# A softplus series moved to VectorE, an early table load and four longer delays in a hybrid layer

## The chip, the cores and the metric

The kernel runs on one NeuronCore of a Trainium2 chip. The metric is device time in microseconds (us), the median of repeated executions. A profile is one execution taken by the hardware profiler.

## The reference

One layer of a hybrid model for 512 prompt tokens and 64 sampled tokens (8 sequences of 8), width 1024, in float32. Three mixers share one input projection: a gated delta rule (4 heads), a differential attention (4 heads) and a pooling mixer. A convolutional feed-forward network follows. Cut to what the change touches:

```python
h = rmsnorm(x, norm_mix)
proj = jnp.einsum('bld,de->ble', h, w_in)
aq, ak, av, az, aa, ab, bq, bk, bv, cx = split_cols(proj, IN_WIDTHS)
qkv, new_conv = causal_dwconv(jnp.concatenate([aq, ak, av], axis=-1), conv_buf, a_conv_w, a_conv_b)
qkv = jax.nn.silu(qkv)
g = -jnp.exp(a_log) * jax.nn.softplus(aa + a_dt_bias)
beta = jax.nn.sigmoid(ab)
o_a, new_delta = gated_delta_rule(q, k, v, g, beta, delta_s0)
# differential attention: softmax of two score maps, their difference times v
mixed = jnp.concatenate([o_a, o_b, o_c], axis=-1)
x = x + jnp.einsum('ble,ed->bld', mixed, w_out)
f, new_ffn = conv_ffn(rmsnorm(x, norm_ffn), ffn_buf, ffn_up, ffn_conv_w, ffn_conv_b, ffn_down)
```

The softplus is max(y, 0) + log(1 + exp(-|y|)). The kernel works out the logarithm as a series: with t = exp(-|y|) and z = t / (t + 2), it is 2z (1 + z²/3 + z⁴/5 + ... + z¹⁶/17).

## The kernel before

**Gemms.** All 576 tokens stand as columns. Each float32 product is three fp32r products of high and low parts: `w_hi` with the high part of x, `w_hi` with its low part, `w_lo` with its high part, each in two pieces of 256 and 320 columns. "A product" in this text is one such matmul. A weight block of 512 KB is fetched by SyncE (`w_raw`), rounded to `w_hi` by ScalarE (line 174) and subtracted to `w_lo` by VectorE (line 175). A gemm result (`g`) has one of two PSUM buffers.

**The order of TensorE** is written by hand. The gemms form the main stream. Side work is written as generators. A virtual clock adds a time for every matmul, and a generator that yields a number is taken up again when that clock has advanced by so many nanoseconds. So a yield says how many products stand between two pieces of side work. All matmuls are kept in program order. On VectorE, ScalarE, GpSimd and SyncE a scheduler orders the instructions by its own simulated timeline, except where the program pins them.

**The start** (`first_products`, lines 334 to 382). x comes in four pieces of two row tiles. For each piece ScalarE makes `wide` (hi) and VectorE its low part; ScalarE squares it (`sq`) and VectorE adds the squares into `total`. The first two weight blocks come in a small part (two row tiles) and the rest. TensorE runs 16 matmuls on ones at the very start, then 96 products of the first two output tiles, then five small matmuls of `total` with ones (the token sums), then products with `wab`, the weights of the decay. From the token sums come `r5`, five diagonal tiles `dg`, `rstd`, and with it everything behind the projection.

**The decays** (`decays`, lines 462 to 506). From a 128x20 tile y the series above is worked out, then `gt`, which TensorE multiplies with triangular constants. Exponentials of the results (`dec`, `gsum`) gate the delta rule. `gsum` goes through device memory (`gsum_d`) into the tile `XT` of each head. The polynomial is a loop of seven multiply-and-add pairs on GpSimd (lines 483 and 484). `yield 11000` stands in front of the matmuls of `gt`.

**The fronts** (`front`, line 553 on), one per delta head: transposes of k, squares into `kt`, a yield, transposes of q and v, then five products of k with k and q whose results VectorE scales into `U`.

**The inversion and the levels** (`invert`, line 611; `levels`, line 647). All heads' 32x32 blocks are inverted on VectorE in 31 multiply-and-subtract pairs (lines 631 and 633). The result goes through device memory (`inv`) and comes back per head as `Xc`. VectorE transposes it into `XTc`, which has one buffer, and four ScalarE copies put it into the diagonal of `XT` (line 666). Two heads at a time, TensorE multiplies `Xc` with `U` into `Y`, and after a yield `Y` with `XT`, whose negated results ScalarE copies into `X64` and `XT` (line 651).

**The attention values** (`values`, line 963): one to four transposes of a score tile, a ScalarE copy `wt` (line 970), a yield, then the products with v. The psm pool has four banks for all side work.

Of the kernel before, what the change touches and what calls it, by code (L numbers as in the profile page):

```python
# [9 lines left out]
F32 = mybir.dt.float32  # L10
F32R = mybir.dt.float32r
AF = mybir.ActivationFunctionType
ALU = mybir.AluOpType
AX = mybir.AxisListType

P = 128
D = 1024
KT = D // P
NP = 512
NS = 64  # L20
T = NP + NS
# [38 lines left out]
def hybrid_step(ctx: ExitStack, tc: tile.TileContext, I, O):  # L60
    nc = tc.nc
# [185 lines left out]
    epst = const.tile([P, 20], F32, name="mhalf")  # L247
# [12 lines left out]
    def col(nm, i):  # L260
        return par[:, off[nm] + i:off[nm] + i + 1]
# [24 lines left out]
    sp = startstack.enter_context(tc.tile_pool(name="start", bufs=1, side="right", reuse_waits="tile"))  # L286
    xs = [sp.tile([P, 2, T], F32, name=f"x{j}") for j in range(KT // 2)]
    raws = []

    def load_first(queue, parts):  # L290

        for w in range(2):
            if len(raws) <= w:
                raws.append((wp.tile([P, 8, P], F32, name="w_raw"), next(sources)))
            raw, src = raws[w]
            queue.dma_start(raw[:, parts], src[:, parts])
# [4 lines left out]
    load_first(nc.scalar, slice(0, 2))  # L301
    load_first(nc.sync, slice(2, 8))
# [32 lines left out]
    def first_products():  # L335
# [4 lines left out]
        def split_first(r):  # L340
            for w in range(2):
                nc.scalar.copy(his[w][:, r], raws[w][0][:, r])  # L342
                nc.vector.tensor_sub(los[w][:, r], raws[w][0][:, r], his[w][:, r].bitcast(F32))  # L343

        ps = [psg.tile([P, 1024], F32, name="g") for _ in range(2)]
        total = None
        for j in range(KT // 2):
            if j < 2:
                split_first((slice(0, 2), slice(2, 8))[j])
            for k in (2 * j, 2 * j + 1):  # L350
                x = xs[j][:, k % 2]
                hi, lo = hmix[k]
                nc.scalar.activation(hi, x, AF.Identity, scale=col("norm_mix", k))
                last_lo[0] = nc.vector.scalar_tensor_tensor(lo, x, col("norm_mix", k), hi.bitcast(F32),
                                                            op0=ALU.mult, op1=ALU.subtract).ins
                for w in range(2):
                    for i, (a, b) in enumerate(((his, hi), (his, lo), (los, hi))):
                        for r in PARTS:
                            mm(ps[w][:, O0:O1][:, r], a[w][:, k], b[:, r], start=k + i == 0,
                               stop=k == KT - 1 and i == 2)  # L360
            sq = sp.tile([P, 2, T], F32, name="sq", bufs=2)
            nc.scalar.activation(sq.rearrange("p k t -> p (k t)"), xs[j].rearrange("p k t -> p (k t)"), AF.Square)
            if total is None:
                total = sp.tile([P, T], F32, name="total")
                nc.vector.tensor_add(total, sq[:, 0], sq[:, 1])
            else:
                for k in range(2):
                    nc.vector.tensor_add(total, total, sq[:, k])
# [92 lines left out]
    def decays(abT):  # L461
# [11 lines left out]
        z = ab.tile([P, 5, HEADS], F32, name="z")  # L473
# [3 lines left out]
        nc.gpsimd.tensor_scalar_add(t2, t1, 2.0)  # L477
        nc.vector.reciprocal(t2, t2)
        nc.gpsimd.tensor_mul(z, t1, t2)
        nc.gpsimd.tensor_mul(z2, z, z)  # L480
        nc.vector.tensor_scalar(t1, z2, 1.0 / 17, 1.0 / 15, op0=ALU.mult, op1=ALU.add)
        for d in (13, 11, 9, 7, 5, 3, 1):
            nc.gpsimd.tensor_mul(t1, t1, z2)  # L483
            nc.gpsimd.tensor_scalar_add(t1, t1, 1.0 / d)  # L484
        nc.vector.scalar_tensor_tensor(t1, t1, 2.0, z, op0=ALU.mult, op1=ALU.mult)
# [7 lines left out]
        yield 11000  # L493
# [17 lines left out]
    with ExitStack() as ctx2:  # L511
# [41 lines left out]
        def front(h):  # L553
# [19 lines left out]
            yield 1530  # L573
# [75 lines left out]
        def levels(pair, inv):  # L649
# [30 lines left out]
            yield 1070  # L680
# [192 lines left out]
        def attention():  # L873
# [90 lines left out]
            def values(a, j, pr):  # L964
# [6 lines left out]
                yield 400 + nk  # L971
# [381 lines left out]
```

## Time and profile before

| | us |
|---|---|
| median of 3 runs (855.42 to 856.59) | 855.6 |
| the profiled execution | 856.47 |
| its span | 854.7 |
| TensorE busy | 835.0 (98%) |
| VectorE busy | 534.3 (63%) |
| ScalarE busy | 357.3 (42%) |
| GpSimd busy | 116.1 (14%) |

The span runs from the first to the last instruction of the execution. The chain that ended last is TensorE for 89% of the span, VectorE for 4%, DMA and ScalarE for 2% each, GpSimd for 1%. TensorE's idle time adds up to 11.4 us by the view of waits. [...]

### The profile page before, as it was taken

What the parts mean: (1) busy time and instruction counts of PE and PEld (TensorE: products, weight loads), DVE (VectorE), ACT (ScalarE), POOL (GpSimd) and SP (SyncE); (2) the same over time, 40 slices, a digit from 0 to 9 for tenths busy, and PEclk for the clock granted to TensorE, in tenths of its full rate; (3) what the DMA queues carried; (4) which work ended last, traced back from release to release, by engine and by line L of the source; (5) the groups of instructions that cost most, each with busy time, mean ns of one, the idle gap of its engine ahead of it and who ended that gap; (6) DMA issues with size and microseconds to landing.
All of it is one profiled execution on the core that took longest, in us unless ns stands there. A gap on an engine that the chain in (4) does not pass through costs nothing.

```text
span 854.7 us, 15955 instructions
## 1 busy us (share of the span) xinstructions
PE 835.0 (98%) x6350; PEld 809.0 (95%) x6350; DVE 534.3 (63%) x1189; ACT 357.3 (42%) x789; POOL 116.1 (14%) x183
## 2 busy tenths in 40 slices
PE   9969999999999999999999999999999999999996
PEld 8969999999999888889999999999999999999996
DVE  7748876884347677774867767667667673323422
ACT  6336563144444455552544344343343442222322
POOL 3332310210002000000012112112121120000001
PEclk9989999999999999999999999999999999999998
DMA  6232222242113432425822222222222223333413
GB/s 245 75 100 78 79 79 77 94 123 77 41 60 94 162 102 67 131 81 170 293 72 78 90 84 75 99 76 80 93 76 97 77 69 111 86 103 86 122 58 111
DMA packets 39033, 84.83 MB, mean 99 GB/s; under 512 B 9387, under 2 KB 14527, under 8 KB 38959
## 3 DMA queue, kind: packets, MB, share of 16 engines
q1 hardware_dynamic: 37870, 82.31, 30.1%
q10 hardware_dynamic: 1088, 1.51, 0.5%
q8 instruction: 50, 0.82, 0.4%
q14 instruction: 25, 0.20, 0.1%
HBM read 72.98 MB, written 10.82 MB: 98 GB/s over the span
## 4 chain that ended last, share of the span: by engine, by line
PE 89%; DVE 4%; DMA 2%; ACT 2%; POOL 1%; issue 1%; POOLq 0%; SPq 0%; DVEq 0%; ACTq 0%
PE g L85 75%; PE m L85 11%; PE m L89 3%; DVE w_lo L175 1%; DMA XT<-gsum_d 1%; ACT w_hi L174 0%; DMA inv<-kq 0%; DMA w<-x_d 0%; DMA x<-in_xT_dram 0%; POOL t L484 0%; POOL t L483 0%; POOL osc L267 0%; DVE oatt L991 0%; DMA Xc<-inv 0%; DVE stat L950 0%
## 5 line engine op out<-in xcount | busy, mean ns | idle before, releaser
L85 PE MATMUL g<-wide,w_hi 128*128 128x256 f32 x1472 | 267.4, 302 | 0.9 <-ACT w_hi L342 0.6
L85 PE MATMUL g<-t,w_hi 128*128 128x256 f32 (+1 forms) x1408 | 242.7, 294 | 0.0
L85 PEld LDWEIGHTS g<-wide,w_hi 128*128 128x128 f32 x1472 | 224.0, 191 | 4.6 <-issue 1.3
L85 PEld LDWEIGHTS g<-t,w_hi 128*128 128x128 f32 x1408 | 210.2, 188 | 0.0
L174 ACT CAST w_hi<-w_raw 128x1024 fp32r<-128x1024 f32 (+2 forms) x109 | 110.6, 1016 | 169.2 <-PE g L85 158.8
L85 PE MATMUL g<-wide,w_lo 128*128 128x256 f32 x736 | 161.7, 302 | 0.2 <-DVE w_lo L343 0.2
L175 DVE TENSOR_TENSOR w_lo<-w_raw,w_hi 128x1024 fp32r<-128x1024 f32 (+2 forms) x109 | 128.2, 1177 | 46.5 <-ACT w_hi L174 45.2
L85 PE MATMUL g<-t,w_lo 128*128 128x256 f32 x704 | 150.4, 295 | 0.0
L85 PEld LDWEIGHTS g<-wide,w_lo 128*128 128x128 f32 x736 | 124.2, 191 | 2.3 <-issue 0.9
L85 PEld LDWEIGHTS g<-t,w_lo 128*128 128x128 f32 x704 | 117.4, 188 | 0.1
L1215 POOL COPY fout<-u 128x4 f32<-128x4 f32 x44 | 51.2, 1164 | 223.1 <-DVE u L1206 223.1
L1212 DVE SCALAR_TENSOR_TENSOR c<-u,par,c 128x511 f32<-128x511 f32 (+3 forms) x176 | 78.9, 511 | 2.5 <-ACT c L1208 2.5
L1206 DVE TENSOR_TENSOR u<-g,rstd 128x576 f32<-128x576 f32 x44 | 33.3, 758 | 59.8 <-PE g L85 58.3
L85 PE MATMUL g<-w,w_hi 128*128 128x256 f32 (+1 forms) x280 | 48.4, 295 | 0.0
L85 PEld LDWEIGHTS g<-w,w_hi 128*128 128x128 f32 x280 | 42.0, 188 | 0.0
L1208 ACT ACTIVATE c<-u,par 128x576 f32<-128x576 f32 x44 | 38.3, 870 | 4.2 <-DVE u L1206 1.4
L1232 ACT ACTIVATE s<-c 128x576 f32<-128x576 f32 x22 | 15.1, 687 | 46.0 <-DVE c L1214 46.0
L267 POOL TENSOR_TENSOR osc<-sso,mhalf 128x5 f32<-128x5 f32 x8 | 9.4, 1182 | 179.6 <-DVE sso L772 62.3
L85 PE MATMUL g<-w,w_lo 128*128 128x256 f32 (+1 forms) x140 | 29.9, 294 | 0.0
L1143 ACT ACTIVATE junk<-m 128x128 f32<-128x128 f32 (+1 forms) x40 | 10.9, 274 | 43.7 <-PE m L89 35.3
L1144 DVE TENSOR_TENSOR t<-m,nf 128x128 f32<-128x128 f32 (+1 forms) x40 | 11.2, 289 | 23.7 <-ACT junk L1143 23.7
L85 PE MATMUL g<-kq,w_hi 128*128 128x256 f32 (+1 forms) x128 | 23.4, 301 | 0.0
(314 smaller groups left out, 1026.3 us busy)
## 6 DMA issues: line engine op xcount, KB each, us to landing
w_raw<-in_ffn_up_dram SPq DMA_DIRECT2D x44, 512.0 KB, 3.2
w_raw<-in_w_in_dram SPq DMA_DIRECT2D x30, 512.0 KB, 3.3
w_raw<-in_ffn_down_dram SPq DMA_DIRECT2D x16, 512.0 KB, 3.5
w_raw<-in_w_out_dram SPq DMA_DIRECT2D x8, 512.0 KB, 3.6
w_raw<-in_ffn_down_dram SPq DMA_DIRECT2D x8, 384.0 KB, 3.2
xr<-in_xT_dram SPq DMA_DIRECT2D x8, 288.0 KB, 3.5
x_d<-xr SPq DMA_DIRECT2D x8, 288.0 KB, 2.1
w<-x_d SPq DMA_DIRECT2D x8, 288.0 KB, 5.8
```

Source lines behind the costliest of these rows:

```text
L85: ordered(nc.tensor.matmul(out, lhsT=lhsT, rhs=rhs, start=start, stop=stop), n / 2.4 if rhs.dtype == F32R else max(54, n / 0.6))
L89: ordered(nc.tensor.transpose(out=out, in_=in_, identity=identity), 107)
L174: nc.scalar.copy(hi[:, :kt], raw)
L175: last_split[0] = nc.vector.tensor_sub(lo[:, :kt], raw, hi[:, :kt].bitcast(F32)).ins
L267: nc.gpsimd.tensor_tensor(out, x, epst[:x.shape[0], :x.shape[1]], op=ALU.pow)
L1143: nc.scalar.activation(junk[:n], src, AF.Square, scale=D ** -0.5, accum_out=op["part"][:n, c, m:m + 1])
L1144: nc.vector.tensor_mul(op["yt"][c][m // 4][:n, (m % 4) * P:(m % 4 + 1) * P], src, op["nf"][:n, m * P:(m + 1) * P])
L1206: nc.vector.tensor_mul(u, ps[:, O0:O1], rstd)
L1208: nc.scalar.activation(c, u, AF.Identity, scale=fw[:, 2, t:t + 1], bias=col("ffn_conv_b", t))
L1212: nc.vector.scalar_tensor_tensor(c[:, a + d:b], u[:, a:b - d], fw[:, j, t:t + 1], c[:, a + d:b], op0=ALU.mult, op1=ALU.add)
L1215: nc.gpsimd.tensor_copy(fout[:, :, :, t], u[:, NP - 64:].rearrange("p (s c) -> p s c", c=64)[:, :, 62:])
L1232: nc.scalar.activation(s, cv[0], AF.Silu)
```

## The change

At the start a copy of one column is put on ScalarE behind its first DMA issues, so that the table load stands in front of it and no longer in front of the first `wide`. ScalarE's first casts and squares are pinned in program order: hi of the first row tile, the small casts, hi of the second, the large casts, and the squares of a piece behind the hi parts of the next. The series runs on VectorE: seven fused add-and-multiply steps replace the seven pairs on GpSimd, and the steps in front of and behind them are rewritten. Four yields change: 11000 to 6500 (`decays`), 1530 to 2600 (`front`), 1070 to 1900 (`levels`), 400 + nk to 1000 + nk (`values`).

```diff
     load_first(nc.scalar, slice(0, 2))
+    nc.scalar.copy(epst[:, :1], epst[:, :1])
     load_first(nc.sync, slice(2, 8))
...
-                nc.scalar.copy(his[w][:, r], raws[w][0][:, r])
+                tc.keep_in_program_order(nc.scalar.copy(his[w][:, r], raws[w][0][:, r]))
...
+        total = sp.tile([P, T], F32, name="total")
+
+        def add_squares(j):
+            sq = sp.tile([P, 2, T], F32, name="sq", bufs=2)
+            tc.keep_in_program_order(nc.scalar.activation(sq.rearrange("p k t -> p (k t)"),
+                                                          xs[j].rearrange("p k t -> p (k t)"), AF.Square))
+            if j == 0:
+                nc.vector.tensor_add(total, sq[:, 0], sq[:, 1])
+            else:
+                for k in range(2):
+                    nc.vector.tensor_add(total, total, sq[:, k])
+
         for j in range(KT // 2):
-            if j < 2:
-                split_first((slice(0, 2), slice(2, 8))[j])
             for k in (2 * j, 2 * j + 1):
                 x = xs[j][:, k % 2]
                 hi, lo = hmix[k]
-                nc.scalar.activation(hi, x, AF.Identity, scale=col("norm_mix", k))
+                tc.keep_in_program_order(nc.scalar.activation(hi, x, AF.Identity, scale=col("norm_mix", k)))
...
+                if k < 2:
+                    split_first((slice(0, 2), slice(2, 8))[k])
...
+            if j:
+                add_squares(j - 1)
+        add_squares(KT // 2 - 1)
...
-        nc.gpsimd.tensor_scalar_add(t2, t1, 2.0)
+        nc.vector.tensor_scalar_add(t2, t1, 2.0)
         nc.vector.reciprocal(t2, t2)
-        nc.gpsimd.tensor_mul(z, t1, t2)
-        nc.gpsimd.tensor_mul(z2, z, z)
-        nc.vector.tensor_scalar(t1, z2, 1.0 / 17, 1.0 / 15, op0=ALU.mult, op1=ALU.add)
-        for d in (13, 11, 9, 7, 5, 3, 1):
-            nc.gpsimd.tensor_mul(t1, t1, z2)
-            nc.gpsimd.tensor_scalar_add(t1, t1, 1.0 / d)
-        nc.vector.scalar_tensor_tensor(t1, t1, 2.0, z, op0=ALU.mult, op1=ALU.mult)
+        nc.vector.tensor_mul(z, t1, t2)
+        nc.vector.tensor_mul(z2, z, z)
+        nc.vector.tensor_scalar_mul(t1, z2, 1.0 / 17)
+        for d in (15, 13, 11, 9, 7, 5, 3):
+            nc.vector.scalar_tensor_tensor(t1, t1, 1.0 / d, z2, op0=ALU.add, op1=ALU.mult)
+        nc.vector.tensor_scalar(t1, t1, 1.0, 2.0, op0=ALU.add, op1=ALU.mult)
+        nc.vector.tensor_mul(t1, t1, z)
...
-        yield 11000
+        yield 6500
...
-            yield 1530
+            yield 2600
...
-            yield 1070
+            yield 1900
...
-                yield 400 + nk
+                yield 1000 + nk
```

**How the order moves.** On TensorE the products stay in their order, and side work moves among them. Between the first decay matmuls (`abT`) and those of `gt` stand 56 products instead of 68, between those and the first transposes of k 42 instead of 30, between these and the transposes of q 22 instead of 14. From there to `Xc` with `U` nothing moves; between `Xc`,`U` and `Y`,`XT` stand 16 instead of 10, and 50 more stand before the second pair. In `values` 12 stand where 6 stood in front of the two-chunk `wt` products.

On VectorE, behind the adds of `total` at the start, before the change:

```order
L368 TENSOR_TENSOR total<-total,sq 128x576
L450 TENSOR_TENSOR lam<-lam 128x1
L368 TENSOR_TENSOR total<-total,sq 128x576
L451 TENSOR_SCALAR lam<-lam 128x1
L453 COPY coef<-lam 64x1
L175 TENSOR_TENSOR w_lo<-w_raw,w_hi 128x1024 x2
L331 TENSOR_SCALAR r_130<-m 128x4
```

The same place with the change:

```order
L458 TENSOR_SCALAR lam<-lam 128x1
L357 TENSOR_TENSOR total<-total,sq 128x576
L460 COPY coef<-lam 64x1
L175 TENSOR_TENSOR w_lo<-w_raw,w_hi 128x1024
L357 TENSOR_TENSOR total<-total,sq 128x576
L175 TENSOR_TENSOR w_lo<-w_raw,w_hi 128x1024
L332 TENSOR_SCALAR r_131<-m 128x4
```

One `w_lo` now stands in front of the last add into `total`; both stood behind it.

On VectorE, around the series, with the change (`t`, `z`, `y` are the 128x20 tiles of the series, `vT` is a convolution of a projected tile, `tmp` its input):

```order
L542 TENSOR_TENSOR tmp<-g,rstd_130 128x512
L543 TENSOR_TENSOR tmp<-g,rstd_130 128x64
L485 RECIPROCAL t_470<-t_470 128x20
L175 TENSOR_TENSOR w_lo<-w_raw,w_hi 128x1024
L486 TENSOR_TENSOR z<-t_469,t_470 128x20
L547 SCALAR_TENSOR_TENSOR vT<-tmp,ah,vT 128x579
L487 TENSOR_TENSOR z_472<-z 128x20
L547 SCALAR_TENSOR_TENSOR vT<-tmp,ah,vT 128x579
L488 TENSOR_SCALAR t_469<-z_472 128x20
L547 SCALAR_TENSOR_TENSOR vT<-tmp,ah,vT 128x579
L490 SCALAR_TENSOR_TENSOR t_469<-t_469,z_472 128x20 x4
L552 SCALAR_TENSOR_TENSOR vT<-tmp,vT 128x579
```

Three more line-490 steps, five steps to `gt` and its memset follow. Before, the same convolution steps stood together, and the seven pairs were on GpSimd beside them.

On VectorE, at the end of the inversion (lines 631 and 633 before, 638 and 640 now), before the change:

```order
L631 TENSOR_TENSOR kq<-a,kq 80x31
L633 TENSOR_TENSOR kq<-kq 80x31
L645 SCALAR_TENSOR_TENSOR a<-tmp,a 128x576 x2
L866 TENSOR_TENSOR kq<-g,rstd_129 128x576
L175 TENSOR_TENSOR w_lo<-w_raw,w_hi 128x1024
```

And with the change:

```order
L873 TENSOR_TENSOR kq<-g,rstd_130 128x576
L638 TENSOR_TENSOR kq<-a,kq 80x31
L175 TENSOR_TENSOR w_lo<-w_raw,w_hi 128x1024
L640 TENSOR_TENSOR kq<-kq 80x31
L652 SCALAR_TENSOR_TENSOR a<-tmp,a 128x576 x4
```

The read of a gemm's result and a `w_lo` now stand in front of the last two inversion steps. On SyncE one fetch of `w_raw` moves in front of the transfer of `inv`.

On ScalarE, in the levels of the first pair (heads 0 and 1 have `XT_2159` and `XT_2173` before, `XT_2162` and `XT_2176` now), before the change:

```order
L666 COPY XT_2173<-XTc_2172 32x5x32 x4
L678 COPY Y_2282<-m_2272 32x160
L666 COPY XT_2388<-XTc_2387 32x5x32
L651 ACTIVATE X64_2160<-m_2302 32x4x32
L651 ACTIVATE XT_2159<-m_2302 32x5x32
```

And with the change:

```order
L673 COPY XT_2162<-XTc_2161 32x5x32 x4
L658 ACTIVATE X64_2163<-m_2311 32x4x32
L658 ACTIVATE XT_2162<-m_2311 32x5x32
L658 ACTIVATE XT_2162<-m_2311 32x4x32
L673 COPY XT_2176<-XTc_2175 32x5x32 x4
```

The second head's four copies into `XT` now stand behind the three copies of the first head's products; before, they stood in front of them.

## Rows read from the trace of the kernel before

**Rows 1.** The page, busy time by engine (share of the span, instructions).

```profile
PE 835.0 (98%) x6350; PEld 809.0 (95%) x6350; DVE 534.3 (63%) x1189; ACT 357.3 (42%) x789; POOL 116.1 (14%) x183
```

**Rows 2.** Waits of TensorE: us in total, times, longest.

```profile
PE m L85 <- DVE gt L492: 5.7, 1, 5.7
PE m L85 <- ACT wt L970: 1.2, 3, 0.4
PE m L89 <- ACT kt L572: 1.1, 1, 1.1
...
PE m L85 <- DVE Y L679: 0.8, 1, 0.8
```

**Rows 3.** Stretches: length, busy time of PE, PEld, DVE, ACT, POOL, granted clock, DMA.

```profile
43.90:49.90 6.00, 0.30 (x3) 0.07 (x2) 3.13 (x10) 1.92 (x2) 4.18 (x18) 0.84 0.03 7
49.90:54.80 4.90, 4.88 (x20) 4.45 (x21) 2.81 (x10) 0.80 (x2) 0.65 (x5) 0.50 0.29 104
...
191.30:194.70 3.40, 3.40 (x21) 3.12 (x20) 3.09 (x9) 2.79 (x10) 0.00 (x0) 0.50 0.00 0
```

**Rows 4.** Timeline of the start: start us, us, engine, line, work, idle before.

```profile
4.22 1.28 ACT L353 ACT_TABLE_LOAD   x1 [4.22 <-DMA x<-in_xT_dram]
...
8.36 0.80 PE L85 MATMUL g<-wide,w_hi 128*128 128x256 f32 x4 [0.64 <-ACT w_hi L342]
...
20.18 0.76 DVE L368 TENSOR_TENSOR total<-total,sq 128x576 f32<-128x576 f32 x1
...
21.12 1.99 ACT L174 CAST w_hi<-w_raw 128x1024 fp32r<-128x1024 f32 x2 [1.53 <-PE g L85]
...
21.98 1.15 PE L85 MATMUL m<-ones,total 128*128 128x1 f32 x10
22.20 2.36 DVE L175 TENSOR_TENSOR w_lo<-w_raw,w_hi 128x1024 fp32r<-128x1024 f32 x2 [1.01 <-ACT w_hi L174]
...
26.32 1.52 PE L85 MATMUL m<-dg,ones 128*128 128x128 f32 x10 [0.31 <-DVE dg L229]
```

**Rows 5.** Timeline of TensorE around gt.

```profile
42.44 0.70 PE L85 MATMUL g<-wide,w_hi 128*128 128x256 f32 x4
...
43.24 0.70 PE L85 MATMUL g<-wide,w_hi 128*128 128x256 f32 x4
...
49.92 1.01 PE L85 MATMUL m<-gt,cst 128*128 128x20 f32 x4 [5.73 <-DVE gt L492]
```

**Rows 6.** Timeline of GpSimd, the last instruction of the series there.

```profile
45.76 0.26 POOL L484 TENSOR_SCALAR t<-t 128x20 f32<-128x20 f32 x1
```

**Rows 7.** Timeline of VectorE beside the series.

```profile
37.84 0.69 DVE L535 TENSOR_TENSOR tmp<-g,rstd 128x512 f32<-128x512 f32 x1 [0.44 <-PE g L85]
...
38.58 0.17 DVE L481 TENSOR_SCALAR t<-z 128x20 f32<-128x20 f32 x1
38.65 1.22 DVE L175 TENSOR_TENSOR w_lo<-w_raw,w_hi 128x1024 fp32r<-128x1024 f32 x1
39.79 2.53 DVE L540 SCALAR_TENSOR_TENSOR vT<-tmp,ah,vT 128x579 f32<-128x579 f32 x3
43.16 0.76 DVE L545 SCALAR_TENSOR_TENSOR vT<-tmp,vT 128x579 f32<-128x579 f32 x1 [0.83 <-ACT tmp L544]
```

**Rows 8.** Timeline of the levels: VectorE, SyncE, ScalarE and TensorE.

```profile
178.29 0.74 DVE L866 TENSOR_TENSOR kq<-g,rstd 128x576 f32<-128x576 f32 x1
...
177.06 0.33 SPq L635 DMA_DIRECT2D inv<-kq  x1
...
181.21 0.94 SPq L662 DMA_DIRECT2D Xc<-inv  x2
...
183.73 1.33 ACT L666 COPY XT<-XTc 32x160 f32<-32x160 f32 x4 [3.93 <-DVE XTc L663]
...
190.41 0.57 ACT L651 ACTIVATE XT<-m 32x160 f32<-32x160 f32 x2
...
185.49 1.02 PE L85 MATMUL m<-Xc,U 32*32 32x32 f32 x36
```

**Rows 9.** DMA issues from 170 to 195 us: KB each, median us to landing.

```profile
Xc<-inv SPq DMA_DIRECT2D x4, 80.0 KB, 2.1
```

More of the change, by code (lines that the diff above doesn't have):

```diff
@@ L341, in split_first @@
             for w in range(2):
-                nc.scalar.copy(his[w][:, r], raws[w][0][:, r])
+                tc.keep_in_program_order(nc.scalar.copy(his[w][:, r], raws[w][0][:, r]))
                 nc.vector.tensor_sub(los[w][:, r], raws[w][0][:, r], his[w][:, r].bitcast(F32))
         ps = [psg.tile([P, 1024], F32, name="g") for _ in range(2)]
-        total = None
+        total = sp.tile([P, T], F32, name="total")
[8 more added lines that the diff above has]
+                    nc.vector.tensor_add(total, total, sq[:, k])
         for j in range(KT // 2):
-            if j < 2:
-                split_first((slice(0, 2), slice(2, 8))[j])
             for k in (2 * j, 2 * j + 1):
@@ L360, in first_products @@
                                stop=k == KT - 1 and i == 2)
[L361 to L368, printed above, removed]
+            if j:
+                add_squares(j - 1)
+        add_squares(KT // 2 - 1)
         with tc.issue_after(last_lo[0]):
```

## The prediction

> **What bounds the kernel now.** I read the page's busy shares first: TensorE works 98% of the span [rows 1], so only its idle time and its slow stretches can be taken away. The view of waits, TensorE alone, gives the idle time by cause [rows 2]: one wait of 5.7 us for gt on VectorE, 1.2 us in three pieces for wt on ScalarE, 1.1 us for kt on ScalarE, 0.8 us for Y on VectorE. The view by stretches then shows the granted clock [rows 3]: 0.84 over the 6.0 us before gt comes, 0.50 in the 4.9 us after it, 0.50 again in the 3.4 us after the wait for Y. [...] So the four places that the change touches behind the start hold 5.7 + 1.2 + 1.1 + 0.8 + 2.45 + 1.7 = 12.95 us, and the start holds the 0.64 us in front of the first product [rows 4]. All else is product after product: six matmuls in 0.80 us [rows 5], 0.133 us each.
>
> The profiled execution took 856.47 us, 0.87 above the median of 855.6. I sum against 856.47 and take 0.87 off at the end.
>
> **The start.** Removed: the table load (1.28 us) between x and the first hi, and the square in front of the first casts [rows 4]. TensorE is free at 8.36 - 0.64 = 7.72, so the first product gains at most 0.64. The 96 products need 16 x 0.80 = 12.8 us, so they end at 20.5 at the earliest; if only the 0.64 counts, at 21.98 - 0.64 = 21.34. I take 20.6, because the gaps behind the first products go with the earlier casts. But the order of VectorE puts the first 128x1024 w_lo subtraction in front of the last add into total, and the token sums on TensorE wait for that add. The w_hi cast that feeds this w_lo starts 0.86 before the products end (21.12 against 21.98), w_lo starts 1.08 behind the cast's start and takes 1.2, the add 0.76 [rows 4]. From 20.6 that is 19.74 + 1.08 + 1.2 + 0.76 = 22.8, against 21.98 before. So the 0.64 is gained, a wait of some 2.2 us is made, and the sums start 0.8 later. Queued behind that add on VectorE are the second w_lo and r5; the decay products fill TensorE until dg, and the 0.31 for which it waited at dg before goes. Net: +0.5 us, from -0.3 to +1.3 (the latter from 21.34).
>
> **The series.** Before, it runs on GpSimd: its last instruction starts at 45.76 [rows 6], and behind it VectorE puts a tmp pair and a w_lo into the rest, so that gt is read at 49.92 [rows 5]. Now TensorE comes 12 products sooner (56 instead of 68 between the two decay steps): 49.92 - 5.73 = 44.19, less 12 x 0.133, is 42.59. VectorE's new order takes up the series around the tmp step that starts at 37.84 and is held by the end of a gemm on TensorE [rows 7]. From there VectorE's new order has the pair of tmp (0.74 to the next start), one w_lo (1.14), three vT convolution steps (2.53 together), one 0.76 add step and fifteen 20-column steps [rows 7]. A 20-column step takes 0.17 there; I take 0.20 from start to start in a dependent chain, and a few overlap a convolution: 2.8 in all. 37.84 + 0.74 + 1.14 + 2.53 + 0.76 + 2.8 = 45.8. TensorE waits 3.2 instead of 5.73, a saving of 2.5. What was on GpSimd costs nothing there. Bounds: if every small step waits 0.3, gt comes 1.5 later (saving 1.0); if the convolutions hide the small steps entirely, 2.8 earlier than 45.8, TensorE hardly waits (saving 5.3). The nearest row is VectorE's own 0.17, so 2.5.
>
> Of the 2.45 us at half clock behind gt I give back 1.0: the 0.84 over 6.0 us says that the clock was at its lower level for the last 1.9 us of the wait [rows 3], and the wait is now shorter by more than that; against it, the wait for Y was 0.8 us long and a half-clock stretch followed. Ends: 0 and 2.45. [...] Series: -2.5 - 1.0 = -3.5, from -1.0 to -7.
>
> **The front delay.** 42 and 22 products stand where 30 and 14 stood, 20 x 0.133 = 2.7 us more before the transposes that need kt, so the wait of 1.1 [rows 2] goes. What is late next: the first head's key products, whose buffers wait for U on VectorE; VectorE now does tmp, w_lo and three convolution steps (0.74 + 1.14 + 2.53) [rows 7] just ahead of them. I charge 0.7 of it, the rest lies beside 20 products. -0.4, from -1.1 to +0.6. The other three heads waited for nothing.
>
> **The levels delay.** 16 products instead of 10 between Xc,U and Y,XT take 0.8 us, just the wait for Y. But the order has moved around it. On VectorE the last inversion step stood directly in front of inv's transfer at 177.06; now the 128x576 step that starts at 178.29, behind a gemm's end, and a w_lo stand ahead of it [rows 8], so inv leaves at 178.29 + 0.74 + 0.2 + 1.2 + 0.2 = 180.6, with a 512 KB fetch ahead of it on SP. From inv's issue at 177.06 to that of Xc at 181.21 are 4.15 us, and Xc takes 2.1 to land [rows 9]; the products of Xc began at 185.49 without a wait [rows 8]. Now Xc is there at 180.6 + 4.15 + 2.1 = 186.9 or later, while TensorE comes to it 8 products later than before (20 more at kt, 12 fewer at gt), 185.49 + 8 x 0.133 = 186.6. I charge 0.9, since the fetch shares the DMA engines with inv. Second, on ScalarE the second head's four XT copies (1.33) [rows 8] have moved behind three negated copies that wait for the first head's Y,XT products (0.57 for two of them, so some 0.8): 0.8 + 1.33, less what overlaps, is a wait of 2.0 in the middle of the pair. New waits 2.9, removed 0.8: +2.1; the half-clock stretch stays. I take +2.0. If both moves are harmless, -0.8 - 1.7 = -2.5; if the fetch delays inv by its own length again and a second stretch of 1.7 follows, +5.
>
> **The values delay.** Twelve products instead of six between the transposes and the wt products: 0.8 us more, against waits of 0.39 each [rows 2]. All three go: -1.2. Against: a psm bank is held 0.8 longer in every chunk and there are four; ends -1.7 and +1.0.
>
> **Sum:** 0.5 - 3.5 - 0.4 + 2.0 - 1.2 = -2.6. 856.47 - 2.6 = 853.9, less 0.87: 853.0 us.
>
> **The rivals.** (1) The moves in the levels stage are hidden: XT's copies are done while TensorE has other work, and the half-clock stretch behind Y goes. For it: 16 products cover more than the old wait. Against it: a copy that stands behind another engine's result in ScalarE's order cannot be early. The levels term is then -2.5, the start is 0, the front -1.1: -8.3, so 847.3.
> (2) Slower: the levels stage becomes a new long wait. The late inversion, the transfer behind the 512 KB fetch and the copies behind the first head's products add up, the clock falls there for longer, +5 instead of +2; it decides once the stage loses more than the other terms' 4.6. With the series at its poor end of -1.5 for lack of clock: 0.5 - 1.5 - 0.4 + 5 - 0.7 = +2.9, so 858.5. For it: both moves stand in the order. Against it: 16 and 50 products stand near by.
> (3) The new wait at the start brings a half-clock stretch of its own, priced at the 1.7 of the stretch behind Y, and gt's stretch stays whole: 0.5 + 1.7 - 2.5 - 0.4 + 2.0 - 1.2 = +0.1, no change, 855.7. For it: 0.8 us of wait was enough at Y. Against it: TensorE was at full clock for all the products before. [...]
> (4) The change does not do what it says: gt's wait merely moves, since VectorE fills the saved time with its queue; that is the poor end of the series, and lies in (2) and (3).
>
> **How the numbers follow.** The forecast has 0.45, and its own range is 850.5 to 855.5; (1) has 0.13, (2) 0.21, (3) 0.21. No change means within 0.2%, 1.7 us, about what a measurement of this kernel can tell. Of the forecast 0.36 falls below 853.9 and 0.09 between; (1) is faster; (2) is slower with 0.19 and same with 0.02; (3) is same with 0.16, faster with 0.03 and slower with 0.02. Faster 0.52, same 0.27, slower 0.21. The range of 847 to 859 reaches from (1) to (2) and leaves out what lies beyond either.
>
> **What would show it.** The wait of the sums for total, near 2.2 us, on VectorE behind w_lo. gt's wait near 3 us, and a shorter stretch at 0.50. No wait for kt; small ones for U. A wait of 1 us or less at Xc and one near 2 at the second head's Y,XT, for XT on ScalarE. No waits for wt on ScalarE. The prediction is wrong if the levels stage loses nothing or more than 4 us, or if gt's wait stays above 4.5.

## The result and the profile after

The changed kernel is slower: 865.1 us median of 4 runs (862.5 to 867.8) against 856.1 of the kernel before in the same comparison; ratio 1.0105, 95% interval 1.0071 to 1.0138. 853.0 us were forecast, with a range of 847 to 859. The profiled execution took 865.19 us, its span is 863.3, against 856.47 and 854.7; the granted clock over the span is 0.985, against 0.991.

TensorE's waits after the change, from the view of waits (us in total, times, longest):

```profile
PE m L85 <- DVE gt L499: 3.2, 1, 3.2
PE m L89 <- ACT p L961: 2.0, 1, 2.0
PE m L85 <- DVE total L357: 2.0, 1, 2.0
PE m L85 <- DVE U L766: 1.6, 1, 1.6
PE m L85 <- ACT XT L673: 1.6, 1, 1.6
PE m L85 <- DVE wide L1007: 1.2, 2, 0.6
...
PE m L85 <- DMA Xc<-inv: 0.2, 1, 0.2
```

They answer to [rows 2]. gt's wait is 3.2 instead of 5.7, and the waits for wt, kt and Y are gone, as they were meant to be. In their place stand total, XT, U (of the scan), p and wide (of the attention). The stretches show the second half of the loss, the columns as in [rows 3]:

```profile
24.20:27.60 3.40, 3.40 (x15) 3.38 (x16) 1.33 (x8) 0.00 (x0) 1.18 (x1) 0.50 0.80 242
48.10:54.90 6.80, 6.80 (x29) 6.35 (x29) 2.37 (x10) 2.14 (x3) 1.12 (x1) 0.50 0.08 22
195.10:205.30 10.20, 10.20 (x58) 9.41 (x58) 4.70 (x9) 5.23 (x13) 1.52 (x6) 0.51 0.25 77
```

The clock column reads 0.50, 0.50 and 0.51. The stretch behind the start's wait is new: in the kernel before the clock is 1.00 from 22 to 36 us. In the one behind gt TensorE works for 6.8 us at half clock, where before it worked for 4.9 us and had spent the first part of the stretch waiting; it costs an estimated 3.4 us (6.8 x 0.50) instead of 2.45 (4.9 x 0.50). The one behind the levels lasts 10.2 us where 3.4 us stood, and costs about 5 us (10.2 x 0.49) where 1.7 us (3.4 x 0.50) were lost. These costs are estimates, the length times what the clock lacks of 1.00, and at the upper end: six products that take 0.80 us at 1.00 [rows 5] take 1.61, 1.44 and 1.44 us at 0.50 (three groups from 49.73 to 54.22 in the changed kernel), so 0.44 to 0.50 of the time is lost.

To see where the time went, I laid both traces side by side by their products: the start of a product, less the start of the same product (by its number) in the kernel before. The table is worked out from the traces, one execution each; about 0.6 us of play is left where side work stands on another side of the product. Kernels other than the changed one are explained in the next section.

| us against the kernel before | behind the start | ahead of Xc | behind the scan | behind the attention | last product |
|---|---|---|---|---|---|
| changed kernel | +2.1 | -0.4 | +5.9 | +8.4 | +8.3 |
| sums_first | -0.7 | -3.0 | +3.3 | +5.8 | +5.9 |
| no_front | +3.7 | -0.7 | -2.0 | +3.2 | +3.1 |
| no_levels | +3.5 | +0.5 | +3.9 | +12.7 | +12.8 |
| no_values | +1.1 | -0.9 | +2.5 | +11.9 | +11.9 |
| only_front | 0.0 | 0.0 | +1.9 | +5.9 | +6.0 |
| only_levels | 0.0 | +0.7 | -0.5 | +8.8 | +8.9 |
| only_values | -0.2 | -0.1 | -1.4 | +0.1 | +1.3 |
| start_series | -0.5 | -3.5 | -5.1 | -5.1 | -5.0 |
| series_late | -0.6 | -1.6 | -3.4 | -3.4 | -3.2 |
| levels_same_length | +0.1 | +0.1 | +2.7 | +2.7 | +3.7 |
| front_same_length | -0.1 | +2.2 | +0.8 | +0.8 | +0.8 |
| series_both | -0.8 | +0.4 | -1.7 | -1.6 | -1.6 |
| series_first | -0.7 | -7.0 | -6.8 | -6.9 | -6.8 |
| start_series_values | -0.9 | -3.4 | -3.2 | -1.9 | -1.6 |

The columns hold half-clock stretches as well as waits, and these differ from execution to execution. In the attention there is none in the changed kernel and in only_front (clock 1.00 from 262 to 402 us), 6.8 us in no_front, and two of 3.4 us each in no_levels, no_values and only_levels (clock 0.92 to 0.97 over the 30 and 32 us that hold them); the sum costs some 3 us in each. The stretch of no_front and the first of only_levels, columns as in [rows 3]:

```profile
320.10:326.90 6.80, 6.48 (x27) 5.37 (x28) 2.67 (x8) 2.34 (x9) 0.00 (x0) 0.50 0.00 0
```

```profile
324.10:327.50 3.40, 3.40 (x16) 2.90 (x15) 1.38 (x4) 0.52 (x3) 0.00 (x0) 0.50 0.00 0
```

The three places as the changed kernel's timeline has them (columns as in [rows 4]). The start, VectorE and TensorE:

```profile
21.16 1.22 DVE L175 TENSOR_TENSOR w_lo<-w_raw,w_hi 128x1024 fp32r<-128x1024 f32 x1 [0.48 <-ACT w_hi L174]
22.30 0.75 DVE L357 TENSOR_TENSOR total<-total,sq 128x576 f32<-128x576 f32 x1
...
23.11 1.31 PE L85 MATMUL m<-ones,total 128*128 128x1 f32 x10 [2.01 <-DVE total L357]
```

VectorE sits idle for 0.48 us for the cast, does w_lo, and only then the last add, for which TensorE waits 2.01 us. The levels: the end of the inversion on VectorE, then ScalarE and TensorE (they answer to [rows 8]):

```profile
177.50 0.76 DVE L873 TENSOR_TENSOR kq<-g,rstd 128x576 f32<-128x576 f32 x1 [0.91 <-PE g L85]
178.18 0.18 DVE L638 TENSOR_TENSOR kq<-a,kq 80x31 f32<-80x31 f32 x1
178.32 1.23 DVE L175 TENSOR_TENSOR w_lo<-w_raw,w_hi 128x1024 fp32r<-128x1024 f32 x1
179.46 0.18 DVE L640 TENSOR_TENSOR kq<-kq 80x31 f32<-80x31 f32 x1
...
191.25 0.57 ACT L658 ACTIVATE XT<-m 32x160 f32<-32x160 f32 x2
191.83 1.33 ACT L673 COPY XT<-XTc 32x160 f32<-32x160 f32 x4
...
192.54 0.34 PE L85 MATMUL m<-Y,XT 32*32 32x32 f32 x5 [1.61 <-ACT XT L673]
```

The inversion has two short steps left when VectorE sits waiting 0.91 us for a gemm's end; its last step starts at 179.46. The second head's XT copies start behind the first head's negated ones, and TensorE waits 1.61 us for them. The attention, TensorE and ScalarE, where the output transposes (oatt) follow four transposes of a score tile:

```profile
325.79 0.66 PE L89 MATMUL m<-cst,p 128*128 128x128 f32 x4
328.46 0.66 PE L89 MATMUL m<-cst,oatt 128*128 128x128 f32 x4 [2.02 <-ACT p L961]
...
327.65 0.67 ACT L961 ACTIVATE p<-m,stat,qscale 128x384 f32<-128x384 f32 x1 [0.53 <-DVE stat L958]
328.22 0.19 ACT L961 ACTIVATION_READ_ACCUMULATOR p<-m,stat,qscale 128x1 f32 x1
```

The transposes of oatt start when the first exponential of the next score tile has ended (327.65 + 0.67, and the read of its sum to 328.41). It reads one of the psm banks, of which the score tile's two maps and its transposes hold three, and oatt's results need two.

### The profile page after: what moved, and what is told of

It reads as the page before. It is cut to its first block, busy times and chain, and to the rows that moved or that the text cites. A ratio compares the mean times of both kernels' runs of the same rounds, so it can differ in the third digit from the quotient of the medians.

```text
span 863.3 us, 15949 instructions
## 1 busy us (share of the span) xinstructions
PE 840.8 (97%) x6350; PEld 814.2 (94%) x6350; DVE 536.4 (62%) x1200; ACT 357.0 (41%) x790; POOL 108.5 (13%) x166
## 4 chain that ended last, share of the span: by engine, by line
PE 92%; DVE 4%; DMA 2%; ACT 2%; issue 1%; ACTq 0%; POOL 0%; SPq 0%; DVEq 0%
PE g L85 77%; PE m L85 12%; PE m L89 3%; DVE w_lo L175 1%; DMA w_raw<-in_w_in_dram 1%; DVE stat L957 1%; DMA inv<-kq 0%; ACT w_hi L174 0%; DMA w_raw<-in_w_out_dram 0%; ACT p L961 0%; DMA Xc<-inv 0%; DVE vT L547 0%; DVE oatt L998 0%; ACT t L1167 0%; DVE m L956 0%
## 5 line engine op out<-in xcount | busy, mean ns | idle before, releaser
L85 PE MATMUL g<-wide,w_hi 128*128 128x256 f32 x1472 | 271.2, 305 | 0.3 <-DVE wide L364 0.3
L85 PEld LDWEIGHTS g<-wide,w_hi 128*128 128x128 f32 x1472 | 226.3, 192 | 3.2 <-issue 0.6
L961 ACT ACTIVATE p<-m,stat,qscale 128x512 f32<-128x512 f32 (+3 forms) x32 | 19.5, 613 | 12.8 <-DVE stat L958 12.8
```

Source lines behind the costliest of these rows:

```text
L85: ordered(nc.tensor.matmul(out, lhsT=lhsT, rhs=rhs, start=start, stop=stop), n / 2.4 if rhs.dtype == F32R else max(54, n / 0.6))
L961: nc.scalar.activation(p_m[:, :nk], maps[m], AF.Exp, scale=qscale[:, j:j + 1], bias=st[:, m:m + 1], accum_out=st[:, 2 + m:3 + m])
```

## The experiments

The kernels ran in groups, each beside runs of the kernel before on the same chip, and each ratio is to those; the median of the kernel before was 856.1 to 857.9 us from group to group. Differences between kernels of different groups are differences of medians, and may be off by a microsecond or two.

**no_front, no_levels, no_values: the changed kernel with one delay taken back.**

```diff
-            yield 2600
+            yield 1530
```

> The changed kernel with the front's yield back at 1530, all else as changed. Theory F: the front's longer delay pushes the end of the inversion behind the end of a gemm, so that a gemm read, a w_lo and a 512 KB fetch get in front of inv, and the second head's XT copies behind the first head's products; then the whole loss of the levels and scan stage (5.7 us between the products ahead of Xc and those behind the scan) goes and the kt wait of 1.1 us comes back: 860 to 861 us, no wait for XT, half clock behind Y for some 3 us as in the kernel before. Theory L: the levels' own longer delay (16 products where 10 stood) makes that loss; then the time gets longer by the kt wait, 866 us.

858.9 us, ratio 1.0013 (0.9995 to 1.0031): 6.2 us below the changed kernel and 1 us below what theory F gave. In the levels its signs are there. The inversion ends before the gemm does, VectorE in the trace of no_front:

```profile
175.97 0.19 DVE L638 TENSOR_TENSOR kq<-a,kq 80x31 f32<-80x31 f32 x1
176.19 0.18 DVE L640 TENSOR_TENSOR kq<-kq 80x31 f32<-80x31 f32 x1
176.30 1.42 DVE L652 SCALAR_TENSOR_TENSOR a<-tmp,a 128x576 f32<-128x576 f32 x2
177.63 0.74 DVE L873 TENSOR_TENSOR kq<-g,rstd 128x576 f32<-128x576 f32 x1
```

There is no wait for XT, and from ahead of Xc to behind the scan the kernel gains 1.3 us where the changed one loses 6.3. Of these 7.6 us some 5 are the long half-clock stretch, which this execution does not have (clock 1.00 from 180 to 222 us). The kt wait did not come back, which I had expected, nor did the 3 us of half clock behind Y. The attention loses 5.2, with the waits of the changed kernel (2.0 for p, 1.2 for wide) and the 6.8 us at half clock shown above.

```diff
-            yield 1900
+            yield 1070
```

> The changed kernel with the levels' yield back at 1070, all else as changed. Theory F: the late inversion and the copies behind the products stay, so does the wait for XT near 1.6 us and the long stretch at half clock: 864 to 867 us. Theory L: the loss of 5.7 us goes and the wait for Y of 0.8 comes back: 859 to 861 us.

868.4 us, ratio 1.0119 (1.0082 to 1.0156). The wait for XT stays at 1.6; theory L is refuted. The half clock behind it lasts 3.4 us in this execution and not 10.2, and the levels and the scan lose 3.4 us instead of 6.3:

```profile
PE m L85 <- ACT XT L673: 1.6, 1, 1.6
```

```profile
194.30:197.70 3.40, 3.40 (x19) 3.12 (x17) 2.54 (x7) 2.85 (x10) 0.00 (x0) 0.50 0.00 0
```

What I had not foreseen: the attention loses 8.8 us (+3.9 to +12.7) where the changed kernel loses 2.5, by waits of 0.9 to 2.0 us and the two half-clock stretches.

```diff
-                yield 1000 + nk
+                yield 400 + nk
```

> The changed kernel with the values' yield back at 400 + nk. Theory V: the longer delay holds the four psm banks longer, and the waits of 2.0, 0.6, 0.6, 0.4 us for banks and for ScalarE's exponentials (p) in the attention stage come from it; the stage lost 3.0 us against the kernel before, so 862 us, with three waits for wt of 0.4 back and none over 0.7. Rival: those waits come from where the heads of the attention now stand, which the front's and the levels' delays move; then 864 to 866 us and the 2.0 wait stays.

871.5 us, ratio 1.0160 (1.0120 to 1.0199). Theory V falls: the 2.0 wait stays (1.9), so it is not the values' delay that makes it. That is what the rival said, but its 864 to 866 us are too low: without that delay the attention is worse, not equal. Its waits:

```profile
PE m L89 <- DVE m L956: 3.9, 4, 1.6
...
PE m L89 <- ACT p L961: 1.9, 1, 1.9
...
PE m L89 <- DVE p L967: 1.6, 1, 1.6
```

**sums_first: the changed kernel with the last add in front of w_lo.**

```diff
-                    nc.vector.tensor_add(total, total, sq[:, k])
+                    last_add[0] = nc.vector.tensor_add(total, total, sq[:, k]).ins
...
-        load_weight()
+        with tc.issue_after(last_add[0]):
+            load_weight()
```

> The changed kernel with one more ordering: the first 128x1024 w_lo is issued on VectorE behind the last add into total. Theory S: the wait of 2.0 us of the token sums and the half clock behind it (the products restart 2.1 us later than in the kernel before) both come from the w_lo in front of that add; then the sums start behind the products, the wait falls under 0.3, no stretch at half clock follows before gt, and the products restart 0.5 to 1.0 us earlier than in the kernel before: 861.5 to 862.5 us. Rival: the adds themselves are late, since VectorE is busy all along; then the wait stays over 1 us and the gain is under 1 us.

861.3 us, ratio 1.0051 (1.0032 to 1.0071), 3.8 below the changed kernel. VectorE and the stretch behind the start:

```profile
20.76 0.76 DVE L358 TENSOR_TENSOR total<-total,sq 128x576 f32<-128x576 f32 x1
21.44 2.35 DVE L175 TENSOR_TENSOR w_lo<-w_raw,w_hi 128x1024 fp32r<-128x1024 f32 x2
```

```profile
22.00:36.00 14.00, 14.00 (x106) 13.28 (x105) 11.56 (x29) 4.21 (x9) 2.57 (x9) 1.00 0.23 77
```

The wait falls to 0.4 (under 0.3 was expected), the clock stays at 1.00, and the products restart 0.7 us earlier than in the kernel before, not 2.1 later. Theory S holds: one w_lo in front of one add made the wait and cost the whole start. That the half clock came from the wait is less sure: no_values has the wait of 2.0 and no half clock behind it (1.00 from 22 to 36 us).

**only_front, only_levels, only_values: one delay alone in the kernel before.** The edits are single lines of the diff above.

> The kernel before with the front's yield at 2600 and nothing else. Theory F: the delay alone turns the order at the end of the inversion (a gemm read and a w_lo in front of the last two steps, the second head's XT copies behind the first head's negated products); a wait for XT of 1.4 to 2 us, more half clock behind it, against a kt wait of 1.1 us gone: 857.5 to 861 us, slower than before. Rival: the late inversion only costs in company with the other edits; then 854.5 to 856 us.

864.8 us, ratio 1.0100 (1.0071 to 1.0129). Theory F holds and was too small. The delay alone turns VectorE's order:

```profile
177.87 0.76 DVE L866 TENSOR_TENSOR kq<-g,rstd 128x576 f32<-128x576 f32 x1 [0.91 <-PE g L85]
178.54 0.18 DVE L631 TENSOR_TENSOR kq<-a,kq 80x31 f32<-80x31 f32 x1
178.68 1.23 DVE L175 TENSOR_TENSOR w_lo<-w_raw,w_hi 128x1024 fp32r<-128x1024 f32 x1
179.82 0.18 DVE L633 TENSOR_TENSOR kq<-kq 80x31 f32<-80x31 f32 x1
```

and the XT wait is there with no other part of the change:

```profile
PE m L85 <- ACT XT L666: 1.6, 1, 1.6
```

In this execution no half-clock stretch followed it (clock 1.00 from 180 to 222 us), so the levels and the scan lost 1.9; the attention lost another 4.0, with three waits for p, 4.0 us together. It took 862.4 us at a granted clock of 0.994 over the span; the other three executions took 863.8 to 866.5 at 0.987 to 0.990.

> The kernel before with the levels' yield at 1900 and nothing else. Theory P: in the levels stage it does what it is meant to (no wait for Y, 0.8 us less, perhaps no half clock behind it), but it puts 12 more products ahead of the attention, whose heads then meet the gemms elsewhere: the output transposes of head 0 come right behind the four transposes of a score tile, all four psm banks are held, and a wait of about 2 us for ScalarE's exponentials arises there, with further waits of 0.6 to 1.6 us per head: 857 to 863 us, the levels stage 0.8 to 2.5 us faster and the attention stage 3 us or more slower. Rival L: the levels stage itself gets slower by 2 us or more. Rival 0: nothing but the 0.8 changes: 854 to 856 us.

864.8 us, ratio 1.0096 (1.0068 to 1.0124), more than the 857 to 863 that were expected. Theory P: the levels and the scan gain 1.2 us (+0.7 to -0.5; this execution has no half-clock stretch there, with 1.00 from 180 to 222 us; it was worth an estimated 1.7 in the kernel before), and the attention loses 9.3, with the very waits of no_values for m and p:

```profile
PE m L89 <- DVE m L949: 3.9, 4, 1.6
PE m L89 <- ACT kt L572: 2.0, 1, 2.0
PE m L89 <- ACT p L954: 1.9, 1, 1.9
...
PE m L89 <- DVE p L960: 1.6, 1, 1.6
```

In both kernels TensorE has the score transposes of head 1, then the transposes of oatt with no product between, then the products with cv.

> The kernel before with the values' yield at 1000 + nk and nothing else. Theory V1: the three waits for wt (1.2 us) go and no wait over 0.6 comes: 854.5 to 856 us. Theory V2: the longer hold of psm banks makes waits in the attention that exceed the 1.2: slower, 858 to 862 us, and the waits name p, m or wide in the attention's lines.

858.7 us, ratio 1.0015 (0.9995 to 1.0035): no difference that can be told. The wt waits go; two for p come, 1.1 us together, and waits of 1.2 for wide (at 312 us, within the attention) and w (at 403 us, behind it). V1 and V2 are each half right.

**levels_same_length, front_same_length: a delay made longer and the next one shorter.**

```diff
-            yield 1070
+            yield 1900
...
-            yield 1470
+            yield 840
```

> As only_levels (the levels' yield at 1900 in the kernel before), with the next yield of the levels cut from 1470 to 840, so that 16 and 8 products stand where 10 and 14 did and all that follows meets the gemms where it did before. Theory P: the loss of only_levels in the attention (9 us between the products behind the scan and those behind the attention) comes from the 12 products by which the attention was moved; then it goes whole: 854.5 to 857 us, no wait over 0.5 in the attention, no wait for Y. Rival: it comes from something else that the longer yield does (banks held, the scheduler's order behind it); then 861 to 865 us.

855.45 us, ratio 0.9993 (0.9978 to 1.0008). The attention's loss is gone: +2.7 behind the scan, +2.7 behind the attention, no wait over 0.4 there. So the shift made it: in only_levels and in the changed kernel the first transposes of a score tile stand behind 1574 products, here and in the kernel before behind 1560, counted in the traces. No gain is left either: TensorE still waits 0.4 for Y, and in the profiled execution (860.1 us, the longest of ten) a half-clock stretch as long as that of the changed kernel stands in the levels, with no wait for XT in front of it:

```profile
191.50:201.70 10.20, 10.20 (x58) 9.41 (x57) 5.20 (x11) 5.90 (x17) 1.53 (x6) 0.50 0.08 26
```

```diff
-            yield 1530
+            yield 2600
...
-            yield 2300
+            yield 1230
```

> As only_front (the front's yield at 2600 in the kernel before), with the next yield of the front cut from 2300 to 1230, so that 22 and 12 products stand where 14 and 20 did and the inversion is spawned where it was. Theory F: the loss of only_front comes from the later inversion and all behind it; then no wait for XT, levels and attention as in the kernel before, the kt wait of 1.1 us gone: 854.5 to 856.5 us. Rival: the shorter second yield brings the first head's transposes of v and its products in front of the weights that they wait for, a new wait of 1 us or more per head: 858 us or more.

857.8 us, ratio 1.0028 (1.0012 to 1.0044). The levels and the attention are as before (no XT wait; +0.8 from the scan to the end), which is what theory F says. But the fronts lose 2.3 us (-0.1 to +2.2, with the kt wait gone among them), with waits of 1.3 for U and 0.6 for squares of q: the rival was right in kind.

**start_series, series_late, series_both, series_first: what the change can give.** start_series is the kernel before with sums_first's start and the series with its yield at 6500. series_late has 11000 there. series_both adds the two cuts above to series_late.

> The kernel before with the start's edit, the added order that puts the last add into total in front of w_lo, and the series on VectorE with its yield at 6500; the front, levels and values yields as before. Theory S with F and P: the start gains 0.7 to 0.9 us, the series 2.5, nothing behind moves: 851.5 to 853.5 us, the fastest kernel of this study. Rival: the scheduler's order behind the decays moves for the series as well, so that new waits of 2 us or more come in the levels or the attention: 855 us or more.

853.1 us, ratio 0.9956 (0.9939 to 0.9973): start and series without the three other delays beat the kernel before. Behind gt's 3.2 only old waits are left (kt 1.2, wt 1.2, Y 1.0).

> As start_series, but the yield in front of gt's matmuls back at 11000, so that TensorE's order is that of the kernel before throughout. Theory: gt's time is set by VectorE's row of steps, not by where TensorE asks for it; 12 more products (1.6 us) then stand in front of the same gt: wait 1.6 instead of 3.2 us, less half clock behind it, 850.5 to 852 us, 1.6 under start_series or a little more. Rival: the longer yield lets the scheduler put more work ahead of the series, gt comes later by the same 1.6 and the wait stays at 3 us: 853 us.

854.4 us, ratio 0.9979 (0.9962 to 0.9995). The rival was right in kind and too small: gt came 3.4 us later than in start_series, and its wait was 5.2. VectorE, from the series' fifth step on:

```profile
43.44 0.17 DVE L492 SCALAR_TENSOR_TENSOR t<-t,z 128x20 f32<-128x20 f32 x1
43.64 0.69 DVE L544 TENSOR_TENSOR tmp<-g,rstd 128x512 f32<-128x512 f32 x1
...
44.47 1.22 DVE L175 TENSOR_TENSOR w_lo<-w_raw,w_hi 128x1024 fp32r<-128x1024 f32 x1
...
47.40 0.82 DVE L549 SCALAR_TENSOR_TENSOR kq<-tmp,ah,kq 128x579 f32<-128x579 f32 x1
...
48.58 0.06 DVE L501 MEMSET gt<- 64x4 f32 x1
```

With 12 more products TensorE ends the next gemm before gt, and the read of that gemm, a w_lo and three convolution steps go in among the series' steps.

> As series_late with the two cuts of front_same_length and levels_same_length: each delay lengthened where TensorE waited, and the next one cut by as much. If the parts add up: 3.5 to 4 us for start and series, 1.6 for the products ahead of gt, 1.1 for kt, 0.8 to 2 for Y: 848 to 850 us, the fastest. If a part's order turns with the others (late inversion, XT copies, attention), 853 us or more, with the wait that names it.

855.4 us, ratio 0.9986 (0.9972 to 1.0001). The parts do not add up: ahead of Xc it stands at +0.4 where series_late has -1.6, so the fronts lose 2 us here too, with waits of 1.2 for U.

series_first is series_late with the reads of the next gemm results issued behind gt:

```diff
-        nc.vector.memset(gt[64:, 4], 0.0)
+        last_gt[0] = nc.vector.memset(gt[64:, 4], 0.0).ins
...
-            nc.vector.tensor_mul(u[:, GAP:GAP + NP], ps[:, O0:O0 + NP], rstd1[:, :NP])
-            nc.vector.tensor_mul(u[:, GAP + SO:], ps[:, O0 + NP:O1], rstd1[:, NP:])
+            with tc.issue_after(last_gt[0]) if last_gt[0] else nullcontext():
+                nc.vector.tensor_mul(u[:, GAP:GAP + NP], ps[:, O0:O0 + NP], rstd1[:, :NP])
+                nc.vector.tensor_mul(u[:, GAP + SO:], ps[:, O0 + NP:O1], rstd1[:, NP:])
```

> As series_late (yield 11000, TensorE's order that of the kernel before), and on VectorE the reads of the next gemm results are issued behind gt's memset, so that the series runs in one row with one w_lo in it. Theory: the chain itself is short (some 4 us from its exponential on, gt by 42 us) and gt was late for the convolution steps among it; then the wait for gt goes under 0.3 us and no half clock follows: 848.5 to 850.5 us. Rival 1: the chain itself is as long, the wait stays over 1.5 us: 852 us or more. Rival 2: the reads that were pushed back make the next gemm or the first head's keys wait, so that what gt gives comes back as waits for g, U or kt of 2 us or more: 852 to 854 us.

849.0 us, ratio 0.9907 (0.9872 to 0.9942), the fastest of the study. The series in one row on VectorE, and the stretches where the half clock stood in [rows 3]:

```profile
39.30 1.46 DVE L493 SCALAR_TENSOR_TENSOR t<-t,z 128x20 f32<-128x20 f32 x7
...
41.68 0.06 DVE L502 MEMSET gt<- 64x4 f32 x1
```

```profile
43.90:49.90 6.00, 6.00 (x46) 5.76 (x46) 6.00 (x16) 2.88 (x11) 3.06 (x10) 1.00 0.28 92
49.90:54.80 4.90, 4.33 (x34) 4.10 (x32) 1.38 (x4) 4.47 (x20) 0.00 (x0) 1.00 0.71 182
```

gt is there at 41.7, TensorE does not wait for it, and the clock stays at 1.00. Rival 2 took a part: waits of 1.1 for vT and 1.5 for kt came in the first front.

> As start_series, with the values' yield at 1000 + nk: the changed kernel with only the order of the last add put right and the front's and the levels' yields as before. If the start's order, the front and the levels are the whole loss: 852 to 855 us, as start_series within 1.7 us, no wait over 0.7 in the attention. If the values' delay costs something of its own: 857 us or more.

855.1 us, ratio 0.9969 (0.9947 to 0.9991). It is the changed kernel with the add in order and the front's and levels' yields as before, and 10 us below it: these three together are the loss. Against expectation a wait of 1.2 for wide stands within the attention, which loses 1.3 us here.

## Why the prediction was wrong, step by step

Forecast and measured terms, the latter from the table's columns:

| term | said | measured |
|---|---|---|
| start | +0.5 | +2.1 |
| series and front, up to Xc | -3.9 | -2.5 |
| levels, with the scan | +2.0 | +6.3 |
| values, with the rest of the attention | -1.2 | +2.5 |

**The levels term was the step that failed first, in size and in its owner.** "New waits 2.9, removed 0.8: +2.1; the half-clock stretch stays." The moves were read rightly: the late inversion, the fetch ahead of inv and the XT copies behind the products are all in the trace. The XT wait is 1.6 where 2.0 was said, the wait for Xc 0.2 where 0.9 was charged. Three things were wrong. The stretch did not stay; it grew from 3.4 to 10.2 us, an estimated 3.3 us more (10.2 x 0.49 less 3.4 x 0.50). A wait of 1.6 us in the scan, for U, was not in the sum at all. And both moves, the late inversion and the XT copies, were booked to the levels' delay, though they come from the front's: only_front has them, only_levels and no_front do not. The front's term of -0.4 should have carried them. The forecast treated each delay by the stage in which it stands. A delay also moves everything that is spawned behind it: here the inversion came later, and its last steps fell behind the end of a gemm. What lengthened the half-clock stretch is not shown: with the same wait for XT it lasts 3.4 us in no_levels and is absent in only_front's profile, and without that wait it lasts 10.2 us in levels_same_length's.

**"Twelve products instead of six ... All three go: -1.2" failed for the same reason.** The three waits for wt did go. But the levels' delay moves the attention against the gemms, and its order for TensorE, which was in hand before the run, shows the oatt transposes of head 0 right behind four score transposes. I had gone through the stages where the edits stand and not through the attention's heads. With the attention back in its place (levels_same_length) the loss is nil. The front's delay moves the attention too, if less: only_front and no_levels have its first score transposes behind 1568 products and lose 4.0 and 8.8 us there. The values' delay was no cause: alone it makes no difference, and in the changed kernel it saved some 5 to 6 us (no_values).

**The start was read rightly and priced too low.** w_lo in front of the last add made the wait of 2.0 us where 2.2 was said. Added to it came the half clock, 0.50 over 3.4 us, an estimated 1.7 us, which the prediction had put into rival 3 alone. no_values, with the same wait and no half clock, stands at +1.1. sums_first has neither (0.4 us, and 1.00).

**The series: the wait was right (3.2 said, 3.23 measured), the clock was not.** "Of the 2.45 us at half clock behind gt I give back 1.0": nothing came back. The clock in the old wait was read rightly: in the kernel before it is 1.00 from 43.9 to 47.9 us and 0.50 from 48.0 to 49.9. But no run shows the 2.45 itself, nor the 1.7 of the stretch behind Y: they are estimates, 4.9 and 3.4 us times 0.50 [rows 3]; in their place the runs show products that lose 0.44 to 0.50 of their time, so 2.2 to 2.45 and 1.5 to 1.7. TensorE worked 6.8 us at half clock instead of 4.9, which costs an estimated 0.95 more (1.9 x 0.50); so this step failed in its sign, and with it the -3.9 became -2.5, although the kt wait went and the 0.7 charged for U did not come. In start_series the same wait of 3.2 is followed by less: the clock is 0.93 over 36 to 62 us there and 0.87 in the changed kernel, which makes some 3.6 us at 0.50 against 6.8, so the size varies between executions. The time of gt was set by the convolutions among its steps: series_first shows the chain ready at 41.7 without them. One reading was also off: the last GpSimd step of the series starts at 46.41 in the kernel before, not at 45.76; no term rests on it.

Rival 2 came nearest. It named the levels as the place, and +5 where +6.3 was measured; it too left out the attention. It had 0.21. Rival 3's two conditions, half clock at the start and none given back behind gt, came as well.

What stays open: why the same wait is followed by a half-clock stretch in one execution and by none in another, and why the kt wait went in no_front with the old front delay. Nor was it tried which of the two, the banks or VectorE's order, makes the 1.6 us waits of no_values; that the oatt transposes wait for a bank is argued from the order and not tested.

## What to carry to other kernels

In an order written by hand with delays in a common clock, a longer delay is also a shift of all that follows: compare the order over the whole program, and look for side work that now meets another piece with nothing between, or a chain whose last step now falls behind a gemm's end. Lengthen a delay where TensorE waits and shorten the next by as much, and the shift is gone; neither of the two pairs tried here made the kernel faster (ratios 0.9993 and 1.0028). Where a short chain decides, keep other work out of its row on the engine: series_late and series_first differ in this alone, with ratios of 0.9979 and 0.9907.

## What the runs showed of the hardware

The half clock varied between executions of the same start. no_values, no_front and no_levels have the changed kernel's start with a wait of 2.0 us, and the view of stretches gives, from no_values and then no_front:

```profile
22.00:36.00 14.00, 12.42 (x95) 11.87 (x95) 10.73 (x26) 3.29 (x6) 2.04 (x7) 1.00 0.22 77
```

```profile
22.00:36.00 14.00, 12.78 (x75) 12.41 (x76) 7.78 (x23) 2.62 (x5) 2.04 (x7) 0.76 0.23 75
```

1.00 and 0.76 of full speed behind the same wait; behind the start the two stand at +1.1 and +3.7 in the table. In the changed kernel TensorE was busy for all 10.2 us of the stretch from 195.10 with the clock at 0.51, and so it was in levels_same_length from 191.50, at 0.50.
